# Opening of a decoder trunk's first layer: loads and transposes by token block, squares and their sums one block later

## The chip, the cores and the metric

The kernel runs on one core of a Trainium2 chip. Its time is the device time of one execution in microseconds (us). Three runs of the kernel before gave 2376.44 us as their median, from 2374.88 to 2378.19.

## The reference, cut to what matters

The program is one inference step of a two-layer decoder for 1024 prompt tokens and 8 sample tokens (1032 columns in the kernel), with a model width of 1024. The first layer (layer A) is a gated linear recurrence, and each layer ends in an MLP. What the change touches is the start of layer A and the start of both MLPs:

```
def rmsnorm(x, g):
    y = xf * lax.rsqrt(jnp.mean(xf * xf, axis=-1, keepdims=True) + EPS)
    return (y * g.astype(jnp.float32)).astype(x.dtype)

h = rmsnorm(x, g_mix[layer])
q, f, i, g = jnp.split(h @ w_in, [hk, 2 * hk, 2 * hk + hv], axis=-1)
forget = lb + (1.0 - lb) * jax.nn.sigmoid(f.astype(f32))
log_f = jnp.log(forget)          # lb comes from a_lb
...
x = x + sq_relu_mlp(rmsnorm(x, g_mlp[layer]), w_up[layer], w_down[layer])
```

The kernel moves the gain g into the weights and multiplies by the root R of the mean square after the product, since R is one number per token.

## The kernel before, in words

Activations lie with features on partitions and tokens in the free dimension. A float32 product is made of three float32r products of upper and lower parts: upper weight by upper activation, lower weight by upper, upper weight by lower. The upper part is made by ScalarE (ACT) as a rounded copy, the lower by VectorE (DVE) as the difference. A "job" is one 128-column block of a weight against all 1032 tokens: 8 slices k by 3 products are 24 steps, each of three matmuls of 344 columns (72 matmuls). One job reads one weight tile of 512 KB (`wr`), which becomes 16 parts in the tile `w` (lines 190 and 191; 195 and 198 where there is no gain).

The order of PE, DVE and ACT is written out by hand: each engine works through its list in the order in which the Python code calls it. `mix_at` (line 344) walks the steps of a job and calls the items of a side list at their step numbers; after each step it takes one waiting weight part from `pend`. So an item with number 8 stands on its engines before step 8.

The opening (lines 873 to 901) runs thus. SP loads four blocks of x (128 tokens by 1024, 512 KB each, tile `xin`), the first weight, four more blocks, the eight sample rows and the second weight. ACT issues the loads of five rows of gains and `a_lb` (tile `setup`). PE turns the gains (line 879) and then x: `turn_x(part, k)` (line 493) makes four transposes of feature slice k into one PSUM bank, ACT and DVE make its parts (lines 503, 504). Part 0 is tokens 0 to 511, part 1 is 512 to 1023, part 2 the samples. The first job (z, the forget gate of head 0) begins with a third of its columns (`z_first`), which need part 0 alone; `z_rest` does the others. The second job is q, the third is v.

`token_stats` (line 522) gives R: ACT squares each token block of `xin` and adds up along the row (line 532), DVE puts the sums on a diagonal (`dg`, line 538), PE multiplies the diagonal by a constant matrix (line 554), ACT takes exp(-0.5 ln) (lines 435, 436) and DVE refines it in three operations (lines 429 to 431). In the kernel before, four blocks are squared in `z_rest` and five in q, and the sums, `bounds` (lines 509 to 520) and `biases` (lines 145 to 159, matmuls for attention tables of layer B) stand in q at steps 10 to 15. The z tile is copied out by ACT and multiplied by R later (line 622); q and v are multiplied by R as DVE empties PSUM (line 614). `gates` (sigmoid line 677, forget line 681, logarithm 685, keys 690, scan 694) stands in v.

Before each MLP, `last_pass` gives eight row blocks y; `done(m)` (line 950) returns for each one its parts, its square (line 951) and the running sum of squares (line 956). Those of the last block run in the first MLP job, beside `rstd_steps`: three sums on PE (line 468), two roots on ACT, two refinements on DVE. The third sum uses the spare half of a PSUM tile whose other half takes the job's third chunk.

A counter of finished transfers is waited for before it is used again: eight counters serve the transfers that SP and ACT issue, in the order of the code.

Of the kernel before, what the change touches and what calls it, by code (L numbers as in the profile page):

```python
# [17 lines left out]
P = 128  # L18
# [24 lines left out]
def trunk(ctx: ExitStack, tc: tile.TileContext, x_prompt, x_sample, state_hgrn, cache_k, cache_v,  # L43
# [56 lines left out]
    rows, rel = setup[:57, :P], setup[:33, P:P + HB + 2 * P + 1]  # L100
    rbn = setup[:33, 480:480 + P].rearrange("p (i b h) -> p i b h", i=2, h=HB // 2)
    for r0, src in ((0, g_mix), (16, g_mlp), (32, a_lb)):
        S.dma_start(out=rows[r0:r0 + 16], in_=src.rearrange("l (k p) -> (l k) p", p=P))
    S.dma_start(out=rows[48:56], in_=g_kv.rearrange("(k p) -> k p", p=P))
    S.dma_start(out=rows[56:57], in_=a_gnorm)
    xin = {}

# [7 lines left out]
    for i in range(4):  # L115
        load_x(i)
# [227 lines left out]
    def mix_at(dense, items):  # L344

        items = sorted(items, key=lambda x: x[0])
        for i, step in enumerate(dense):
            while items and items[0][0] <= i:
                items.pop(0)[1]()
            step()  # L350
            if pend:
                pend.pop(0)()
        for _, f in items:
            f()
# [133 lines left out]
    for i in range(4, NBLK + 1):  # L488
        load_x(i)
# [3 lines left out]
    def turn_x(part, k):  # L493
        o = ps()
        if part < 2:
            cs = HALF[part]
            for j in range(4):
                PE.transpose(out=o[:, blk(j)], in_=xin[part * 4 + j][:, blk(k)], identity=ident)
        else:
            cs = slice(SEQ, T)  # L500
            PE.transpose(out=o[:, :NS], in_=xin[NBLK][:NS, blk(k)], identity=ident[:NS, :NS])
        o = o[:, :cs.stop - cs.start]
        S.activation(out=xs[k][0][:, cs], in_=o, func=AF.Copy)
        V.tensor_tensor(out=xs[k][1][:, cs], in0=o, in1=f32(xs[k][0][:, cs]), op=ALU.subtract)
# [103 lines left out]

    def scaled(name, then, late=None):
# [44 lines left out]
    def head_jobs(h, late=None):  # L654
# [3 lines left out]
        def got_f(z):  # L658
            hd.k = z

        def got_q(q):
            hd.q = q

        def got_v(v):
            hd.v = v

        return hd, (job(xs, scaled("z", got_f, late)) + job(xs, scaled("q", got_q))
                    + job(xs, scaled("v", got_v)))
# [204 lines left out]
    for h in range(H):  # L873
        late = [] if h == 0 else None
        hd, dense = head_jobs(h, late)
        if h == 0:
            z_first, z_rest = first_job(scaled("z", lambda z: setattr(hd, "k", z), late))
            o = ps()
            PE.transpose(out=o[:, :57], in_=rows, identity=ident[:57, :57])
            V.tensor_copy(out=cols, in_=o[:, :57])  # L880
            want_w(1)
            for k in range(NK):
                turn_x(0, k)
                pend.pop(0)()
            for k, f in enumerate(z_first):
                f()
                if k > 4:
                    turn_x(1, k - 5)
            for k in range(NK):
                if k > 2:  # L890
                    turn_x(1, k)
                turn_x(2, k)
            squares, diagonal, sums, refine = token_stats()
            mix_at(z_rest, spaced(squares[:4], 11, 25) + spaced(diagonal[:3], 15, 25))
            side = spaced(squares[4:], 0, 7) + spaced(diagonal[3:], 1, 9)
            side += list(zip((10, 10.1, 10.2, 11, 12.5, 12.6), sums + refine))
            side += [(1, load_biases), (14, bounds), (15, biases), (20, lambda: late[0]())]
            mix_at(dense[3 * NK:6 * NK], side)
            loads.close()
            mix_at(dense[6 * NK:], spaced(gates(hd), 1, 20))  # L900
# [32 lines left out]
    def last_pass(ins, ys, g=None):  # L933
# [11 lines left out]
        def done(m):  # L945
# [11 lines left out]
            if m == NK - 1:  # L957
                return [(1, square), (2, upper), (3, total), (5, lower)]
# [117 lines left out]
    def mlp(layer, ys, side, final=None):  # L1076
# [25 lines left out]
        for g in range(NG):  # L1102
            us, rs, pairs = [], [], []
            quads = g < NG - 1
            for e in mlp_order(g):
# [16 lines left out]
                if g == 0 and n == 0:  # L1122
                    spare = []
                    dense = job(xs, up_evac(rs), spare=spare)
                    at = side + list(zip((7.5, 8, 8.5, 9.5, 10, 10.5, 12), stats.rstd_steps(spare)))
# [456 lines left out]
```

## Time and profile before

| | |
|---|---|
| median of three runs | 2376.44 us |
| the profiled execution | 2374.52 us |
| its span, first to last instruction | 2372.8 us |
| PE busy | 2322.2 us, 98% of the span |
| DVE busy | 1622.6 us, 68% |
| ACT busy | 937.9 us, 40% |
| mean granted clock of TensorE | 0.995 |

The profiled execution is one run of the program with the hardware profiler. Its times count from the start of the span. PE is busy nearly all the time, so what costs time is where it waits, and where its granted clock is 0.50 (1.2 GHz) and not 1.00 (2.4 GHz). Idle time of another engine matters only where PE waits for it. A number in square brackets at the end of a timeline row is the idle time of the engine just before, and what ended it.

### The profile page before, as it was taken

The numbers are of one execution on the slowest core, as the hardware profiler recorded it, in microseconds if no ns is written. First come the engines' busy times: TensorE is split into PE (matmuls) and PEld (weight loads), VectorE is DVE, ScalarE is ACT, GpSimd is POOL, SyncE is SP. The second block draws the span as 40 slices with busy tenths as digits, with TensorE's granted clock in tenths as the row PEclk, the third lists the DMA queues.
The fourth block names the chain that finished last, engine by engine and source line by source line (L and its number), as shares of the span: only waits on it lengthen the run. The fifth ranks groups of instructions, "written<-read, shape, count | busy, mean of one in ns | idle before, by whom it ended". The sixth has DMA issues, their size and how long they took to land. (4 is left out here: it accounts for less than half of the span.)

```text
span 2372.8 us, 40040 instructions
## 1 busy us (share of the span) xinstructions
PE 2322.2 (98%) x16371; PEld 2288.1 (96%) x16371; DVE 1622.6 (68%) x3122; ACT 937.9 (40%) x1911; POOL 207.2 (9%) x209
## 2 busy tenths in 40 slices
PE   7999999999999999999999999999999999999998
PEld 6999999999999999999999989899999999999998
DVE  5766676675567667676676788886477676676765
ACT  6344454553323223223224588753222322322322
POOL 0111111120000000000000134430000000000002
PEclk8999999999999999999999999999999999999999
DMA  3222222226111111111111113011111121111122
GB/s 126 59 69 68 68 65 64 64 63 83 45 45 45 54 45 53 56 45 54 45 54 54 48 38 109 21 35 37 44 54 45 45 57 49 47 54 45 45 63 81
DMA packets 201771, 133.10 MB, mean 56 GB/s; under 512 B 10438, under 2 KB 194928, under 8 KB 201588
## 3 DMA queue, kind: packets, MB, share of 16 engines
q1 hardware_dynamic: 190740, 111.23, 16.0%
q0 software_dynamic: 10496, 18.72, 3.6%
q8 instruction: 129, 2.11, 0.4%
q10 hardware_dynamic: 352, 0.59, 0.1%
q14 instruction: 54, 0.44, 0.1%
HBM read 115.97 MB, written 14.50 MB: 55 GB/s over the span
## 5 line engine op out<-in xcount | busy, mean ns | idle before, releaser
L392 PE MATMUL ps<-h,w 128*128 128x344 f32 (+1 forms) x6096 | 1152.9, 323 | 13.0 <-DVE tmp L430 4.4
L392 PEld LDWEIGHTS ps<-h,w 128*128 128x128 f32 x6096 | 988.1, 189 | 20.7 <-issue 8.8
L392 PE MATMUL ps<-l,w 128*128 128x344 f32 (+1 forms) x3048 | 656.1, 323 | 0.0
L392 PEld LDWEIGHTS ps<-l,w 128*128 128x128 f32 x3048 | 509.1, 189 | 1.1 <-issue 0.2
L1072 DVE TENSOR_TENSOR y<-ps,y 128x516 f32<-128x516 f32 x392 | 271.6, 693 | 125.0 <-PE ps L1067 123.0
L1081 DVE SCALAR_TENSOR_TENSOR r<-ps,R 128x688 f32<-128x688 f32 x126 | 81.7, 690 | 213.3 <-PE ps L392 213.3
L1067 PE MATMUL ps<-l,w 128*128 128x258 f32 x1120 | 226.0, 283 | 0.0
L1067 PE MATMUL ps<-b,w 128*128 128x258 f32 x1568 | 225.3, 283 | 0.0
L1067 PE MATMUL ps<-t,w 128*128 128x258 f32 x1344 | 218.1, 284 | 0.0
L228 ACT ACTIVATE w<-wr 128x512 fp32r<-128x512 f32 x168 | 99.3, 623 | 292.2 <-DVE wr L240 218.2
L1087 ACT ACTIVATE r<-r 128x1032 f32<-128x1032 f32 x63 | 67.3, 1068 | 372.9 <-DVE r L1081 372.9
L1067 PEld LDWEIGHTS ps<-b,w 128*128 128x128 f32 x1568 | 205.5, 190 | 0.0
L1067 PEld LDWEIGHTS ps<-t,w 128*128 128x128 f32 x1344 | 184.8, 190 | 0.3
L1067 PEld LDWEIGHTS ps<-l,w 128*128 128x128 f32 x1120 | 173.6, 189 | 0.0
L195 ACT ACTIVATE w<-wr 128x512 fp32r<-128x512 f32 x168 | 102.5, 622 | 132.5 <-PE ps L1067 66.5
L198 DVE TENSOR_TENSOR w<-wr,w 128x512 fp32r<-128x512 f32 x168 | 116.3, 711 | 53.1 <-ACT w L195 53.0
L191 DVE SCALAR_TENSOR_TENSOR w<-wr,cols,w 128x128 fp32r<-128x128 f32 x352 | 131.7, 416 | 29.0 <-ACT w L190 28.1
L236 DVE TENSOR_TENSOR w<-wr,w 128x512 fp32r<-128x512 f32 x168 | 115.4, 687 | 42.7 <-ACT w L228 42.7
L240 DVE TENSOR_TENSOR wr<-wr 128x256 f32<-128x256 f32 x280 | 118.2, 422 | 6.2
L190 ACT ACTIVATE w<-wr,cols 128x128 fp32r<-128x128 f32 x352 | 115.5, 391 | 13.4 <-PE ps L392 12.1
L1022 ACT ACTIVATE t<-r 128x1032 fp32r<-128x1032 f32 x56 | 59.7, 1065 | 91.4 <-DVE r L1044 91.4
L1522 POOL TENSOR_TENSOR sqc<-sqc,sq 128x384 f32<-128x384 f32 (+1 forms) x18 | 16.6, 925 | 748.4 <-ACT sq L1521 748.2
(285 smaller groups left out, 2734.1 us busy)
## 6 DMA issues: line engine op xcount, KB each, us to landing
wr<-in_w_up_dram SPq DMA_DIRECT2D x64, 512.0 KB, 4.1
wr<-in_w_down_dram SPq DMA_DIRECT2D x112, 256.0 KB, 3.1
wr<-in_w_a_in_dram SPq DMA_DIRECT2D x32, 512.0 KB, 4.2
xin<-in_x_prompt_dram SPq DMA_DIRECT2D x8, 512.0 KB, 7.1
si<-in_state_hgrn_dram POOLq DMA_DIRECT2D x8, 512.0 KB, 5.0
vb<-vrows POOLq DMA_DIRECT2D x8, 512.0 KB, 3.9
out_dram<-si POOLq DMA_DIRECT2D x8, 512.0 KB, 4.2
wr<-in_w_a_out_dram SPq DMA_DIRECT2D x8, 512.0 KB, 20.9
```

Of the source, the lines that this page charges most:

```text
L190: S.activation(out=hi[:, j], in_=part[:, j], func=AF.Copy, scale=g[:, k:k + 1])
L191: V.scalar_tensor_tensor(out=lo[:, j], in0=part[:, j], scalar=g[:, k:k + 1], in1=f32(hi[:, j]), op0=ALU.mult, op1=ALU.subtract)
L195: S.activation(out=hi, in_=part, func=AF.Copy)
L198: V.tensor_tensor(out=lo, in0=part, in1=f32(hi), op=ALU.subtract)
L228: S.activation(out=hi, in_=src, func=AF.Copy)
L236: V.tensor_tensor(out=lo, in0=src, in1=f32(hi), op=ALU.subtract)
L240: return lambda: V.tensor_tensor(out=out, in0=in0, in1=in1, op=op)
L392: PE.matmul(st["o"][c], lhsT=ww[:, col:col + P], rhs=xx[:, cs], start=((k, i) == first and also is None), stop=((k, i) == last))
L1067: PE.matmul(o[:, c, :CQ], lhsT=ww, rhs=xx[:, c * CQ:(c + 1) * CQ], start=(begins and k == 0 and i == 0), stop=(k == 1 and i == 2), skip_gr ...
L1072: V.tensor_tensor(out=y, in0=o[:, :, :CQ], in1=y, op=ALU.add)
L1081: V.scalar_tensor_tensor(out=v(r), in0=p, scalar=0.0, in1=v(R), op0=ALU.max, op1=ALU.mult)
L1087: S.activation(out=rs[-1], in_=rs[-1], func=AF.Square)
```

## The change

In the opening: SP issues the first block of x, then the first weight, then seven blocks, the samples and the second weight. ACT issues one row of gains (`first`) before the table load; the others (`load_gains`) stand after the turning of `first`. All parts of the first weight are made before the parts of x. PE turns part 0 block by block, eight transposes from one block into eight banks. Parts 1 and 2 are turned between the steps of `z_first` and `z_rest`. All nine squares stand in q (steps 0 to 8), with `hold=10`, which keeps the parts of v's weight until step 10. The sums, `bounds` and refinements stand in v; z and q are both copied out by ACT and multiplied by R in v; `biases` stands at step 22 of v and the turning of the other gains at step 22 of q.

In both MLPs: the square of the last block moves to step 0, its sum to 2.5, its upper part to 3.5; the three sums stand before step 9 instead of 8 and 9, the roots at 9, the refinements before steps 10 and 11.

```diff
-    for r0, src in ((0, g_mix), (16, g_mlp), (32, a_lb)):
-        S.dma_start(out=rows[r0:r0 + 16], in_=src.rearrange("l (k p) -> (l k) p", p=P))
-    S.dma_start(out=rows[48:56], in_=g_kv.rearrange("(k p) -> k p", p=P))
-    S.dma_start(out=rows[56:57], in_=a_gnorm)
+    first = A(F32, "setup0")[:16, :P]
+    S.dma_start(out=first, in_=g_mix.rearrange("l (k p) -> (l k) p", p=P))
+    def load_gains():
+        for r0, src in ((16, g_mlp), (32, a_lb)):
+            S.dma_start(out=rows[r0 - 16:r0], in_=src.rearrange("l (k p) -> (l k) p", p=P))
+        S.dma_start(out=rows[32:40], in_=g_kv.rearrange("(k p) -> k p", p=P))
+        S.dma_start(out=rows[40:41], in_=a_gnorm)
-    for i in range(4):
-        load_x(i)
+    load_x(0)
...
-            if pend:
+            if pend and i >= hold:
                 pend.pop(0)()
...
-    for i in range(4, NBLK + 1):
+    for i in range(1, NBLK + 1):
         load_x(i)
...
+            gains(first, 0)
+            load_gains()
             want_w(1)
-            for k in range(NK):
-                turn_x(0, k)
-                pend.pop(0)()
+            while pend:
+                pend.pop(0)()
+            half = [ps() for _ in range(NK)]
+            for j in range(4):
+                for k in range(NK):
+                    PE.transpose(out=half[k][:, blk(j)], in_=xin[j][:, blk(k)], identity=ident)
+            for k in range(NK):
+                parts_x(half[k], HALF[0], k)
             for k, f in enumerate(z_first):
                 f()
-                if k > 4:
-                    turn_x(1, k - 5)
-            for k in range(NK):
-                if k > 2:
-                    turn_x(1, k)
-                turn_x(2, k)
+                if k > 3:
+                    turn_x(1, k - 4)
+                    turn_x(2, k - 4)
             squares, diagonal, sums, refine = token_stats()
...
-            side += list(zip((10, 10.1, 10.2, 11, 12.5, 12.6), sums + refine))
-            side += [(1, load_biases), (14, bounds), (15, biases), (20, lambda: late[0]())]
-            mix_at(dense[3 * NK:6 * NK], side)
+            side = spaced(squares, 0, 8) + spaced(diagonal, 1, 9) + [(6, load_biases), (22, lambda: gains(rows, 16))]
+            mix_at(dense[3 * NK:6 * NK], side, 10)
             loads.close()
-            mix_at(dense[6 * NK:], spaced(gates(hd), 1, 20))
+            side = list(zip((0.1, 0.2, 0.3, 1.5, 2, 2.1), sums + refine)) + [(2.2, f) for f in late]
+            side += [(0.4, bounds), (22, biases)]
+            mix_at(dense[6 * NK:], side + spaced(gates(hd), 3.5, 20), 3)
...
             if m == NK - 1:
-                return [(1, square), (2, upper), (3, total), (5, lower)]
+                return [(0, square), (2.5, total), (3.5, upper), (5, lower)]
...
-                    at = side + list(zip((7.5, 8, 8.5, 9.5, 10, 10.5, 12), stats.rstd_steps(spare)))
+                    at = side + list(zip((8.2, 8.3, 8.4, 8.5, 8.6, 9.5, 10.5), stats.rstd_steps(spare)))
```

ACT at the start of the program, before. The five loads into `setup` stand without a wait, and the parts of x (`h`) alternate with those of the first weight (`w`).

```order
L103 DMA setup_73<-in_g_mix_dram 16x128
L103 DMA setup_73<-in_g_mlp_dram 16x128
L103 DMA setup_73<-in_a_lb_dram 16x128
L104 DMA setup_73<-in_g_kv_dram 8x128
L105 DMA setup_73<-in_a_gnorm_dram 1x128
L117 ACT_TABLE_LOAD
L503 ACTIVATE h_119<-ps_162 128x512 [waits PE_49]
L190 ACTIVATE w_160<-wr_105,cols 128x128 [waits DMAHW1_49,DVE_49]
```

The same place in the changed kernel, and below it PE's first transpose of each block of x, which names the counter of that block: blocks 1 to 4 use DMAHW3 to DMAHW6.

```order
L103 DMA setup_2_74<-in_g_mix_dram 16x128
L126 ACT_TABLE_LOAD
L108 DMA setup_73<-in_g_mlp_dram 16x128 [waits DMAHW3_49]
L108 DMA setup_73<-in_a_lb_dram 16x128 [waits DMAHW4_49]
L109 DMA setup_73<-in_g_kv_dram 8x128 [waits DMAHW5_49]
L110 DMA setup_73<-in_a_gnorm_dram 1x128 [waits DMAHW6_49]
L199 ACTIVATE w_161<-wr_96,cols 128x128 [waits DMAHW2_49,DVE_49]
L199 ACTIVATE w_161<-wr_96,cols 128x128 x3
```

```order
L892 MATMUL ps_179<-ident,xin_76 128x128 [waits DMAHW1_49]
L892 MATMUL ps_179<-ident,xin_98 128x128 [waits DMAHW3_49]
L892 MATMUL ps_179<-ident,xin_100 128x128 [waits DMAHW4_49]
L892 MATMUL ps_179<-ident,xin_102 128x128 [waits DMAHW5_49]
L508 MATMUL ps_253<-ident,xin_104 128x128 [waits DMAHW6_49,PE_49]
```

The last four loads of ACT now stand behind the counters of blocks 1 to 4 and ahead of every part of the first weight; PE needs block 4 itself (`xin_104`) only in `z_first`.

DVE in q, before: the small operations of `biases` (lines 147 and 149, on `setup`) follow `bounds`, and z times R (line 622) comes after them.

```order
L520 TENSOR_SCALAR oml<-lb 128x8 [waits DVE_49]
L147 TENSOR_SCALAR setup_73<-setup_73 33x64 [waits DMAHW3_49,DMAHW2_49]
L147 TENSOR_SCALAR setup_73<-setup_73 33x64
L149 TENSOR_SCALAR setup_73<-setup_73 33x16 [waits DVE_49]
L155 COPY bias_s<-ps_554 64x258 [waits PE_49]
L156 COPY nsk<-ps_554 128x16
L159 COPY vrow<-ps_560 16x128 [waits PE_49]
L622 TENSOR_TENSOR z_425<-z_425,R_496 128x1032
```

DVE in v, in the changed kernel: z and q times R (line 637), forget (687), keys (696), the scan (700), and then the same small operations.

```order
L637 TENSOR_TENSOR z_417<-z_417,R_557 128x1032 [waits DVE_49]
L637 TENSOR_TENSOR q_542<-q_542,R_557 128x1032
L200 SCALAR_TENSOR_TENSOR w_549<-wr_547,cols,w_549 128x128 [waits DMAHW1_49,Activation_49]
L200 SCALAR_TENSOR_TENSOR w_549<-wr_547,cols,w_549 128x128 [waits Activation_49] x3
L687 TENSOR_SCALAR z_417<-z_417,oml,lb 128x1032
L200 SCALAR_TENSOR_TENSOR w_550<-wr_547,cols,w_550 128x128 [waits Activation_49] x4
L693 COPY fs_650<-z_417 128x8 [waits DVE_49]
L696 TENSOR_SCALAR z_417<-z_417 128x1032 [waits DVE_49,Activation_49]
L700 SCALAR_TENSOR_TENSOR b_671<-m_137,lf_648 128x1024
L156 TENSOR_SCALAR setup_73<-setup_73 33x64 [waits DMAHW3_49,DMAHW2_49]
L156 TENSOR_SCALAR setup_73<-setup_73 33x64
L158 TENSOR_SCALAR setup_73<-setup_73 33x16 [waits DVE_49]
```

The matmuls of `biases` on PE wait for these operations, and they moved from ahead of the gates to behind the scan.

ACT at the start of the first MLP, before: the upper part of one half of the next weight (`w_5990`) stands ahead of the square of the last block (`sq_5998`).

```order
L951 ACTIVATE sq_5951<-y_5530 128x1032
L195 ACTIVATE w_5990<-wr_5988 128x512 [waits DMAHW2_49,PE_49,Activation_49]
L951 ACTIVATE sq_5998<-y_5576 128x1032 [waits DVE_49,Activation_49]
L195 ACTIVATE w_5991<-wr_5988 128x512 [waits PE_49,Activation_49]
L415 ACTIVATE h_6004<-y_5576,cols 128x1032 [waits Activation_49]
```

The same place in the changed kernel.

```order
L964 ACTIVATE sq_5956<-y_5535 128x1032
L964 ACTIVATE sq_5993<-y_5581 128x1032 [waits DVE_49,Activation_49]
L204 ACTIVATE w_5997<-wr_5995 128x512 [waits DMAHW2_49,PE_49]
L204 ACTIVATE w_5998<-wr_5995 128x512 [waits PE_49,Activation_49]
L425 ACTIVATE h_6018<-y_5581,cols 128x1032 [waits Activation_49]
```

The square and the upper part of the weight changed places. On DVE the order did not change: the lower part of that weight stands before the sum of squares in both kernels.

```order
L955 TENSOR_TENSOR y_5581<-ps_5947,y_5581 128x344 [waits PE_49]
L207 TENSOR_TENSOR w_5997<-wr_5995,w_5997 128x512 [waits DMAHW2_49,Activation_49]
L969 TENSOR_TENSOR sq_5651<-sq_5651,sq_5993 128x1032 [waits DVE_49]
L207 TENSOR_TENSOR w_5998<-wr_5995,w_5998 128x512 [waits Activation_49]
L433 SCALAR_TENSOR_TENSOR l_6023<-y_5581,cols,h_6018 128x1032 [waits DVE_49,Activation_49]
```

So on DVE the sum of squares (line 969) now has, through the lower part ahead of it, the later upper part of ACT as its condition.

## Rows read from the trace of the kernel before

**Rows 1.** Waits of PE, whole program: us in total, times, longest.
```profile
PE ps L392 <- DVE tmp L430: 4.4, 2, 2.2
```
**Rows 2.** Stretches: length, busy time by engine, granted clock (PEclk), DMA.
```profile
44.30:57.90 13.60, 10.12 (x37) 8.93 (x36) 7.33 (x23) 7.05 (x16) 0.00 (x0) 0.50 0.13 38
575.30:579.30 4.00, 0.00 (x0) 0.00 (x0) 3.94 (x5) 0.98 (x2) 0.00 (x0) 1.00 0.51 128
579.40:583.50 4.10, 4.10 (x17) 4.04 (x18) 2.87 (x4) 2.63 (x3) 0.00 (x0) 0.59 0.14 33
1665.60:1669.00 3.40, 2.88 (x10) 2.88 (x11) 0.99 (x2) 0.00 (x0) 0.00 (x0) 0.50 0.00 0
```
**Rows 3.** Waits of SP's DMA queue, 0 to 120 us.
```profile
SPq L111 <- DMA setup<-in_g_mix_dram: 1.6, 1, 1.6
```
**Rows 4.** Timeline of the opening: start, us, engine, line, tiles, count [idle before].
```profile
11.26 6.16 PE L498 MATMUL ps<-ident,xin 128*128 128x128 f32 x29 [1.88 <-DMA xin<-in_x_prompt_dram]
13.08 0.40 ACT L190 ACTIVATE w<-wr,cols 128x128 fp32r<-128x128 f32 x1 [0.71 <-DVE l L504]
13.38 0.58 ACT L503 ACTIVATE h<-ps 128x512 fp32r<-128x512 f32 x1
17.17 0.56 PE L643 MATMUL ps<-h,w 128*128 128x344 f32 x2
26.90 2.44 ACT L190 ACTIVATE w<-wr,cols 128x128 fp32r<-128x128 f32 x8
```
**Rows 5.** Timeline from the squares to the end of v.
```profile
29.25 1.05 ACT L532 ACTIVATE junk<-xin 128x1024 f32<-128x1024 f32 x1
33.84 1.14 ACT L618 ACTIVATE z<-ps 128x344 f32<-128x344 f32 x3
42.39 0.66 ACT L435 ACTIVATE r<-ps,eps_t 128x512 f32<-128x512 f32 x1
43.84 0.69 DVE L429 SCALAR_TENSOR_TENSOR tmp<-r 128x512 f32<-128x512 f32 x1 [0.68 <-ACT r L436]
50.32 1.09 PE L152 MATMUL ps<-setup 33*64 33x129 f32 x4 [3.48 <-ACT w L190]
52.41 2.09 PE L392 MATMUL ps<-h,w 128*128 128x344 f32 x6
52.73 1.21 DVE L622 TENSOR_TENSOR z<-z,R 128x1032 f32<-128x1032 f32 x1
53.97 1.06 ACT L677 ACTIVATE z<-z 128x1032 f32<-128x1032 f32 x1 [3.10 <-DVE z L622]
55.04 1.28 ACT L131 ACT_TABLE_LOAD   x1
59.14 1.36 DVE L614 TENSOR_TENSOR q<-ps,R 128x344 f32<-128x344 f32 x3 [5.20 <-PE ps L392]
61.73 0.81 DVE L681 TENSOR_SCALAR z<-z,oml,lb 128x1032 f32<-128x1032 f32 x1
63.67 2.27 DVE L690 TENSOR_SCALAR z<-z 128x1032 f32<-128x1032 f32 x1 [0.26 <-ACT lf L685]
65.86 2.28 DVE L694 TENSOR_TENSOR_SCAN b<-m,lf 128x1024 f32<-128x1024 bf16 x1
70.48 1.36 DVE L614 TENSOR_TENSOR v<-ps,R 128x344 f32<-128x344 f32 x3 [2.34 <-PE ps L392]
```
**Rows 6.** Timeline of the first MLP's start.
```profile
606.13 0.68 DVE L198 TENSOR_TENSOR w<-wr,w 128x512 fp32r<-128x512 f32 x1
607.41 1.23 DVE L956 TENSOR_TENSOR sq<-sq,sq 128x1032 f32<-128x1032 f32 x1 [0.60 <-ACT sq L951]
607.28 0.61 ACT L195 ACTIVATE w<-wr 128x512 fp32r<-128x512 f32 x1
608.79 1.39 PE L468 MATMUL ps<-sq,ones_d 128*128 128x344 f32 x4 [1.22 <-DVE sq L956]
615.93 0.89 PE L392 MATMUL ps<-h,w 128*128 128x344 f32 x4 [2.23 <-DVE tmp L430]
```

More of the change, by code (lines that the diff above doesn't have):

```diff
@@ L99, in trunk, with gains @@
     setup = A(F32, "setup")
-    rows, rel = setup[:57, :P], setup[:33, P:P + HB + 2 * P + 1]
+    rows, rel = setup[:41, :P], setup[:33, P:P + HB + 2 * P + 1]
     rbn = setup[:33, 480:480 + P].rearrange("p (i b h) -> p i b h", i=2, h=HB // 2)
-    for r0, src in ((0, g_mix), (16, g_mlp), (32, a_lb)):
-        S.dma_start(out=rows[r0:r0 + 16], in_=src.rearrange("l (k p) -> (l k) p", p=P))
-    S.dma_start(out=rows[48:56], in_=g_kv.rearrange("(k p) -> k p", p=P))
-    S.dma_start(out=rows[56:57], in_=a_gnorm)
+    first = A(F32, "setup0")[:16, :P]
+    S.dma_start(out=first, in_=g_mix.rearrange("l (k p) -> (l k) p", p=P))
     xin = {}
+    def load_gains():
[3 more added lines that the diff above has]
+        S.dma_start(out=rows[40:41], in_=a_gnorm)
+    def gains(src, c0):
+        n = src.shape[0]
+        o = ps()
+        PE.transpose(out=o[:, :n], in_=src, identity=ident[:n, :n])
+        V.tensor_copy(out=cols[:, c0:c0 + n], in_=o[:, :n])
     def load_x(i):
@@ L342, in mix, with mix_at @@
             step()
-    def mix_at(dense, items):
+    def mix_at(dense, items, hold=0):
         items = sorted(items, key=lambda x: x[0])
@@ L501, in turn_x, with parts_x @@
             PE.transpose(out=o[:, :NS], in_=xin[NBLK][:NS, blk(k)], identity=ident[:NS, :NS])
-        o = o[:, :cs.stop - cs.start]
+        parts_x(o[:, :cs.stop - cs.start], cs, k)
+    def parts_x(o, cs, k):
         S.activation(out=xs[k][0][:, cs], in_=o, func=AF.Copy)
@@ L607, in trunk, with got @@
         pass
+    def got(hd, key):
+        return lambda t: setattr(hd, key, t)
     def scaled(name, then, late=None):
@@ L656, in head_jobs @@
         hd.h = h
[L658 to L668, printed above, removed]
+        return hd, (job(xs, scaled("z", got(hd, "k"), late)) + job(xs, scaled("q", got(hd, "q"), late))
+                    + job(xs, scaled("v", got(hd, "v"))))
     def gates(hd, other=None):
@@ L876, in trunk @@
         if h == 0:
[L877 to L880, printed above, removed]
+            z_first, z_rest = first_job(scaled("z", got(hd, "k"), late))
+            gains(first, 0)
+            load_gains()
             want_w(1)
+            while pend:
+                pend.pop(0)()
+            half = [ps() for _ in range(NK)]
@@ L893, in trunk @@
-            squares, diagonal, sums, refine = token_stats()
-            mix_at(z_rest, spaced(squares[:4], 11, 25) + spaced(diagonal[:3], 15, 25))
-            side = spaced(squares[4:], 0, 7) + spaced(diagonal[3:], 1, 9)
-            side += list(zip((10, 10.1, 10.2, 11, 12.5, 12.6), sums + refine))
-            side += [(1, load_biases), (14, bounds), (15, biases), (20, lambda: late[0]())]
-            mix_at(dense[3 * NK:6 * NK], side)
+                if k > 3:
+                    turn_x(1, k - 4)
+                    turn_x(2, k - 4)
@@ L899, in trunk @@
+            squares, diagonal, sums, refine = token_stats()
+            for i, f in enumerate(z_rest):
+                f()
+                if i % 3 == 0 and i < 12:
+                    turn_x(1, 4 + i // 3)
+                    turn_x(2, 4 + i // 3)
+                if i > 11 and pend:
+                    pend.pop(0)()
+            side = spaced(squares, 0, 8) + spaced(diagonal, 1, 9) + [(6, load_biases), (22, lambda: gains(rows, 16))]
+            mix_at(dense[3 * NK:6 * NK], side, 10)
             loads.close()
-            mix_at(dense[6 * NK:], spaced(gates(hd), 1, 20))
+            side = list(zip((0.1, 0.2, 0.3, 1.5, 2, 2.1), sums + refine)) + [(2.2, f) for f in late]
```

## The prediction

> **What bounds the kernel now.** I began with the waits of PE and the stretches of low clock, since PE is busy for 98% of the span. A kernel like this loses time in two ways: PE waits, or PE works at 0.50 of its clock. The waits show, in the part that the change touches, the first steps of the two MLPs, 2.2 us each, for the last operation of the root R [rows 1]. The stretches show where the clock is low: from 44.3 to 57.9 us the mean granted clock is 0.50, while PE is busy for only 10.1 of 13.6 us; after a wait of 4.0 us (575.3 to 579.3) it is 0.59 over the next 4.1 us; and in the second MLP's start it is 0.50 for another 3.4 us [rows 2]. Then I read the timelines of the opening, of layer A's first three jobs and of the MLP's start, to see which wait ends last at each point. What follows goes by four marks: S, the first product of the z job (17.17 us before [rows 4]); Z, the end of z (its copy begins at 33.84); the end of v (its first copy begins at 70.48); and the resumption of PE in the MLP (615.93) [rows 5, 6].
>
> **The start, up to S.** The change takes x's parts out of the alternation with the weight's parts and turns x block by block. It also moves ACT's last four small loads ahead of all weight parts, and the order of the changed kernel gives them a wait for the counters of x's blocks 1 to 4. A queue that has to issue a load stands still until the counter is there: SP waited 1.6 us in that way for g_mix [rows 3]. If ACT does the same, no weight part is made before block 4 is there. Block 4 is the sixth large transfer (x0, w0, x1, x2, x3, x4). Before, the fourth one had landed at 11.26 at the latest, since PE began on it then, and the fifth, the weight, at 13.08, when ACT made its first part [rows 4]. So the sixth lies between 13.1 and 13.08 + 1.8 = 14.9; I take the middle, 14.0. From there: 0.3 to pass the waits, the eight upper weight parts 2.44, one upper part of x 0.58 [rows 4], its lower part 0.69 (as the 512-wide DVE operation of [rows 5]). S = 14.0 + 0.3 + 2.44 + 0.58 + 0.69 = 18.0, which is 0.8 later than before; with the ends of the landing, 17.1 to 18.9.
>
> From S to Z stand 72 matmuls and 40 transposes of blocks 4 to 8. The job before v's end had 72 matmuls between the copies of q at 59.14 and of v at 70.48, 11.3 us [rows 5]. A transpose took 6.16 / 29 = 0.21 us in the opening [rows 4]; at the full clock I put it at half, so 40 take 4.0. That is 15.3, and if ACT and DVE hold the transposes back a little, 16.2; I take 15.7. PE has nothing to do for some 3.7 us ahead of S, so the first matmuls may run at the low level; that costs 0 to 1.2, and I take 0.8. Z = 18.0 + 15.7 + 0.8 = 34.5, against 33.8: **+0.7**, bounds -0.7 to +2.0.
>
> **From Z to the end of v.** Before, this took 70.48 - 33.84 = 36.6 us [rows 5]. It held the matmuls of two jobs, a wait of 3.5 us ahead of the matmuls of `biases`, and the 13.6 us at half clock. In the changed kernel the squares and weight parts are apart, and q runs densely: 72 matmuls, v begins at about Z + 12. What is late next is `biases`. Its matmuls now stand on PE ahead of step 22 of v, and the small DVE operations that they read stand on DVE behind the scan, as the order shows. PE can't pass them, and the rest of v, two steps and its copy, is queued behind.
>
> The chain that ends there begins on ACT at Z: copy of z 1.14, nine squares at (33.84 - 29.25) / 4 = 1.15 each (before, four stood between these two rows), 10.3 [rows 5]; eight weight parts of v, 2.44 [rows 4], made behind the squares; copy of q 1.14, four roots and exponentials of 0.66 and 0.8 between them [rows 5]. That is Z + 18.4. Then DVE: six refinements of 0.69 with 1.0 of gaps and the tail of `bounds` 0.5, 5.5 in all, and z times R 1.21, Z + 25.1; on ACT the sigmoid 1.06 and the table load 1.28, and three weight parts 0.9, Z + 28.4; on DVE a lower weight part 0.3, forget 0.81, four more lower parts and the small copy 1.3, keys 2.27, scan 2.28, Z + 35.4, and 0.4 for the three small operations: Z + 35.8 [rows 5].
>
> PE reaches step 22 earlier: 12 to the start of v, 22 steps of 11.3 / 24 = 0.47 are 10.4, the sums of R some 2.2 (six at 1.39 / 4 = 0.35 [rows 6]), and up to 1.0 for a bank; Z + 25.6. So it stands idle for about 10 us, which is a wait that the kernel before doesn't have. The matmuls of `biases` begin at 50.32 and the next products at 52.41, 2.1 later, at half clock [rows 5]; the two steps left are 0.94 at full clock and 1.7 or so at half. After a wait of 4.0 us the clock was low [rows 2], so after 10 I take it as low. End of v: Z + 35.8 + 2.1 + 1.7 = Z + 39.5, against Z + 36.6: +2.9. The job after it starts at the low level too: the loss in the row after the 4.0 us wait is 4.1 x (1 - 0.59), 1.7 us in all [rows 2], of which about 1.2 are spent inside `biases` and the two steps, and 0.5 is left. **+3.4**, bounds +0.9 (the clock doesn't fall) to +4.4.
>
> **The two MLPs.** On ACT the square changes places with an upper weight part (0.61), so the square is ready some 0.6 earlier. The sum of squares on DVE still stands behind the lower part of that weight (0.68), which now waits for an upper part that comes after a 1.1 us square. Before: the upper part, the lower part at 606.13, its end at 606.81, a wait of 0.60 for the square, the sum at 607.41 [rows 6]. After: the square ends 0.6 earlier, at about 606.8; upper part 0.61 and lower part 0.68, then the sum at 608.5 to 608.6, 1.2 later. From the sum on, the chain is what it was: sum's end 607.41 + 1.23 = 608.64, PE resumes at 615.93, 7.3 later [rows 6], and all its links (sums, roots, refinements) are in the change. But PE is now held one step earlier: the refinements stand before steps 10 and 11, and the third chunk that needs the spare half stands at step 11 rather than 12; one step more, 0.47, is left for after. Each opening +1.2 + 0.4 = 1.6, so **+3.2** for two. To this comes the clock: the wait grows from 2.2 to 3.9 us, and the row of the second MLP shows 3.4 us at 0.50, of which PE's 2.88 busy us lose about 1.4 [rows 2]. If the first MLP too falls to that level, another 1.4: I take **+1.4**, bounds 0 to 2.9.
>
> **The sum.** 0.7 + 3.4 + 3.2 + 1.4 = +8.7 us on the profiled execution's own 2374.52, or 2383.2. That execution is 1.9 below the median of the runs shown; against the median it would be 2385.1, and I forecast 2383. What can be told from no change is about 0.2%, 4.75 us: faster is below 2371.7, slower above 2381.2. Nothing else in the program changes its order by a price that I can read; a different place of buffers may add or take 2 us.
>
> **Rivals.** *The loads don't hold ACT.* The row that I go by is of SP; no row shows ACT waiting at an issue. If the waits are passed on, the weight's parts start when the weight lands, at about the landing of the second large transfer, S is set by x's block 3 at 11 to 12 us and its parts, about 15.5, and Z falls by 2.5: 2383.2 - 2.5 = 2380.6. Against it: the loads and the weight parts are in one list of one engine.
>
> The Trainium skill has a sentence on this in "DMA: Bandwidth & Descriptors", section "Anatomy of one DMA", the gpsimd path: "any semaphore wait happens on the issuing sequencer before dispatch." It is written for another path than ACT's; by it the loads hold ACT and the sum stays at 2383, and SP's 1.6 us [rows 3] agree.
>
> *The clock stays full.* Then the terms of the clock go, 0.8 + 0.8 + 0.5 + 1.4 + the 1.2 of `biases` = 4.7: 2378.5. For it: ahead of 575.3 the clock was full, and a wait of 2.2 us in the first MLP is not in the rows of low clock. Against it: the 4.0 us wait was followed by the low level [rows 2], and mine is longer.
>
> *The MLP part does nothing* (the change doesn't do what it says there, the one move being paid by the other): 2383.2 - 4.6 = 2378.6. For it: 0.6 us of DVE's idle time ahead of the sum are free today [rows 6]. Against it: the lower part still has to come first.
>
> *The other side: `biases` holds nobody.* The place is PE's step 22 of v. If the DVE chain is some 10 us shorter than I make it, because squares or weight parts run beside other things in ways my chain puts end to end, it is through when PE gets there at Z + 25.6. The wait, its low clock and the 13.6 us at half clock of before are all gone: v ends at Z + 29, 7.6 earlier than before, and with the opening's +0.7, the MLPs' +4.6 and a full clock the sum is 2374.5 + 0.7 - 7.6 + 4.6 = 2372.2, or 2371 with an early S. It decides from a chain of less than Z + 29: then each us less than that is a gain. Against it: keys, scan, forget, sigmoid and table load alone are 7.7 us [rows 5] behind R, which needs all nine squares behind Z.
>
> **How the numbers follow.** My forecast (+5 to +13 us) has 0.53; the loads rival 0.12, the full clock 0.14, the MLP rival 0.10, the other side 0.11. The forecast lies above 2381.2 in 0.47 and below in 0.06; the loads rival is split in halves; of the full clock and of the MLP rival 0.03 each are slower and the rest is no change; the other side is 0.09 faster, 0.02 no change; and 0.01 of the others may be faster. That makes faster 0.10, no change 0.31, slower 0.59. The range goes from 2375 (the full clock and the MLP rival with 3.5 us off) to 2390 (every bound of the sum at its upper end: 2.0 + 4.4 + 3.2 + 2.9 = +12.5 is 2387, and 2 to 3 more for what the sum doesn't hold).
>
> **What would show it.** In the changed kernel's waits: one of PE for DVE at `biases` in v of about 10 us (under 3 would make the second term wrong and the other side right), and no wait of 3.5 us in q. In its timeline: the first upper weight part at 14 us and S at 18 (S at 15.5 would be the loads rival). In the MLP: PE resuming 1.6 us later, with the wait at 3.9. In the stretches: low clock behind `biases`; a full one would be that rival. A time under 2375 makes the prediction wrong, and most of all its 10 us.

## The result, and the profile after

The changed kernel took 2389.32 us, the median of four runs (2387.8 to 2392.32); the kernel before took 2377.06 in the runs beside it. The ratio is 1.0054, with a 95% interval of 1.0037 to 1.0072: slower, by 9 to 17 us. The profiled execution took 2387.8 us, with a span of 2386.1 against 2372.8.

Waits of PE in the changed kernel (us in total, times, longest); the row of `tmp` answers to [rows 1]:

```profile
PE ps L161 <- issue: 9.7, 1, 9.7
...
PE ps L402 <- DVE y L955: 4.4, 1, 4.4
PE ps L402 <- DVE tmp L440: 4.4, 2, 2.2
PE ps L658 <- DVE l L516: 4.0, 1, 4.0
...
PE ps L402 <- ACT r L445: 2.9, 2, 1.4
```

The 9.7 us stand ahead of the bias matmuls (line 161), where the kernel before waited 3.5 us [rows 5]. The 4.0 us stand ahead of the first product. The profile names "issue" as the cause of the long one: PE's instruction waits for two tiny operations on DVE (line 156), and only the timeline shows what these stood behind.

Timeline of the changed kernel's opening (start, us, engine, line, tiles, count, idle time before and what ended it); these rows answer to [rows 4, 5]. ACTq is the queue from which ACT issues its loads; the first row is the last of its four small ones:

```profile
14.09 0.23 ACTq L110 DMA_DIRECT2D setup<-in_a_gnorm_dram  x1
14.43 2.44 ACT L199 ACTIVATE w<-wr,cols 128x128 fp32r<-128x128 f32 x8 [11.88 <-DMA xin<-in_x_prompt_dram]
18.13 0.94 PE L658 MATMUL ps<-h,w 128*128 128x344 f32 x2 [3.99 <-DVE l L516]
...
38.14 1.10 PE L402 MATMUL ps<-h,w 128*128 128x344 f32 x6
...
50.41 1.05 PE L566 MATMUL ps<-dg,ones_d 128*128 128x128 f32 x8
...
52.74 0.66 ACT L445 ACTIVATE r<-ps,eps_t 128x512 f32<-128x512 f32 x1
...
71.08 2.28 DVE L700 TENSOR_TENSOR_SCAN b<-m,lf 128x1024 f32<-128x1024 bf16 x1
73.28 0.26 DVE L156 TENSOR_SCALAR setup<-setup 33x64 f32<-33x64 f32 x2
...
73.54 1.09 PE L161 MATMUL ps<-setup 33*64 33x129 f32 x4 [9.71 <-issue]
...
77.18 1.36 DVE L629 TENSOR_TENSOR v<-ps,R 128x344 f32<-128x344 f32 x3 [1.17 <-PE ps L402]
...
91.40 1.36 DVE L629 TENSOR_TENSOR z<-ps,R 128x344 f32<-128x344 f32 x3 [5.14 <-PE ps L402]
```

Read it by points that both kernels have. The first product of q stood at 34.08 us before, the copy of the next head's z at 83.06:

```profile
34.08 1.10 PE L392 MATMUL ps<-h,w 128*128 128x344 f32 x6
...
83.06 1.36 DVE L614 TENSOR_TENSOR z<-ps,R 128x344 f32<-128x344 f32 x3 [4.58 <-PE ps L392]
```

So the changed kernel is 4.1 us late when z ends (38.14), 6.7 at v's copy (77.18 against 70.48 [rows 5]) and 8.3 at the next z (91.40). The granted clock explains the odd tenths. Stretches of the changed kernel (length, busy time of PE, PE's loads, DVE, ACT, POOL, then PEclk):

```profile
18.10:23.40 5.30, 5.27 (x20) 5.04 (x20) 4.16 (x7) 2.64 (x6) 0.00 (x0) 0.53 0.53 141
...
73.50:79.00 5.50, 5.46 (x20) 4.65 (x21) 2.61 (x9) 0.40 (x2) 0.00 (x0) 0.50 0.00 0
79.00:82.00 3.00, 3.00 (x15) 3.00 (x15) 1.62 (x5) 2.54 (x8) 0.00 (x0) 0.65 0.02 5
...
627.20:630.60 3.40, 3.40 (x14) 3.40 (x13) 0.00 (x0) 0.00 (x0) 0.00 (x0) 0.51 0.02 5
```

After each of the two long waits PE works at the low level for some microseconds: by the granted clock, 5.3 x 0.47 = 2.5 us are lost behind the first product. The last row is the first MLP, which ran at the full level before. Its timeline, which answers to [rows 6]:

```profile
617.51 1.23 DVE L969 TENSOR_TENSOR sq<-sq,sq 128x1032 f32<-128x1032 f32 x1
...
618.89 1.97 PE L478 MATMUL ps<-sq,ones_d 128*128 128x344 f32 x6 [1.18 <-DVE sq L969]
...
622.60 0.91 PE L402 MATMUL ps<-h,w 128*128 128x344 f32 x4 [1.43 <-ACT r L445]
...
626.02 0.42 PE L402 MATMUL ps<-l,w 128*128 128x344 f32 x1 [2.20 <-DVE tmp L440]
...
633.54 1.30 DVE L1094 SCALAR_TENSOR_TENSOR r<-ps,R 128x688 f32<-128x688 f32 x2 [7.02 <-PE ps L402]
```

Set against the last copy of y ahead of it (604.93 before, 613.90 after), the sum of squares is 1.1 us later, and the first copy of the up product 3.1 later (621.42 before). In the second MLP the same copy moves from 1672.92 to 1686.19, and the copy of y ahead of it from 1655.12 to 1666.67: 1.7. The sum of all: 4.1 + 2.6 + 1.6 + 3.1 + 1.7 = 13.1 of the 13.3 us between the two spans; what comes and goes between (0.6 later at the first output block, 0.6 earlier before the second MLP) cancels.

### The profile page after: what moved, and what is told of

The parts are those of the page before. It is cut to its first block, busy times and chain, and to the rows that moved or that the text cites. A ratio compares the mean times of both kernels' runs of the same rounds, so it can differ in the third digit from the quotient of the medians.

```text
span 2386.1 us, 40037 instructions
## 1 busy us (share of the span) xinstructions
PE 2325.2 (97%) x16372; PEld 2290.4 (96%) x16372; DVE 1620.7 (68%) x3121; ACT 939.2 (39%) x1914; POOL 207.4 (9%) x209
## 5 line engine op out<-in xcount | busy, mean ns | idle before, releaser
L402 PEld LDWEIGHTS ps<-h,w 128*128 128x128 f32 x6096 | 988.5, 189 | 18.1 <-issue 9.6
L200 DVE SCALAR_TENSOR_TENSOR w<-wr,cols,w 128x128 fp32r<-128x128 f32 x352 | 129.0, 410 | 36.8 <-ACT w L199 35.8
```

The lines of the kernel that those rows point to most:

```text
L200: V.scalar_tensor_tensor(out=lo[:, j], in0=part[:, j], scalar=g[:, k:k + 1], in1=f32(hi[:, j]), op0=ALU.mult, op1=ALU.subtract)
L402: PE.matmul(st["o"][c], lhsT=ww[:, col:col + P], rhs=xx[:, cs], start=((k, i) == first and also is None), stop=((k, i) == last))
```

## The experiments

Each run's time is a median, and the ratio is to the kernel before, run on the same chip (2375.8 to 2376.4). The changed kernel was not run again beside them, and the kernel before had given 2377.1 beside it: where a run is set against 2389.3, a difference of 1 to 2 us is not settled by the times, and I go by the trace.

**The MLP part alone, both ways.** In the first run the changed kernel has the MLPs of before; in the second the kernel before has the changed MLPs.

```
-                return [(0, square), (2.5, total), (3.5, upper), (5, lower)]
+                return [(1, square), (2, upper), (3, total), (5, lower)]
...
-                    at = side + list(zip((8.2, 8.3, 8.4, 8.5, 8.6, 9.5, 10.5), stats.rstd_steps(spare)))
+                    at = side + list(zip((7.5, 8, 8.5, 9.5, 10, 10.5, 12), stats.rstd_steps(spare)))
```

> The changed kernel (2389.3 us) with the two MLP openings as they were before; all else as changed. Theory: the moved square makes the sum of squares 1.1 us later, and PE takes up full speed later, 3.1 us in the first MLP and 1.7 in the second; so 4.8 us come back, 2384.5, and the sum starts 2.5 us after the last y again, not 3.6. Rival: in the first MLP the low clock comes from elsewhere (the opening's pushed-back weights), and only the 1.1 us of each is the MLP's; then 2.2 come back, 2387.

> The kernel before (2376) with the MLP part of the change alone. Theory: the sum of squares 1.1 us later in each MLP, and low clock behind PE's longer wait in both: 3.3 in the first and 1.5 in the second, 4.8 in all, 2380.8. Rival: by itself, without the opening, the clock doesn't fall; then 2.2, 2378. It also tells if the two parts of the change add up: 2389.3 less this difference should be what the changed kernel with the old MLPs took, 2387.

Measured: 2387.03 for the first (2381.59 to 2390.58), and 2381.34 for the second (ten runs; ratio 1.0022, 1.0013 to 1.0031). The second settles the size: +4.9 us, with an interval of 3 to 7. Its stretch from 618 to 619 us is at 0.50, so the clock falls without the opening's help. The first run, at 2.3 less than the changed kernel, is scattered over 9 us; its median does not tell 4.8 from 2.2, nor whether the two parts of the change add up. In its profiled execution the first MLP's waits for the sum and the root are 0.7 and 0.5 us, against 1.2 and 1.4 in the changed kernel, and the clock is full in both MLPs. The last row is a stretch of the second one:

```profile
PE ps L402 <- DVE tmp L440: 2.2, 1, 2.2
PE ps L478 <- DVE sq L969: 0.7, 1, 0.7
PE ps L402 <- ACT r L445: 0.5, 1, 0.5
```

```profile
1673.00:1676.50 3.50, 2.04 (x13) 2.04 (x14) 1.82 (x4) 0.00 (x0) 0.00 (x0) 1.00 0.00 0
```

From the last copy of y to the first copy of the up product it takes 16.5 us in each MLP; the changed kernel took 19.6 and 19.5, the kernel before 16.5 and 17.8. So in this execution 6.1 us came back, 1.3 of them because the second MLP stayed at the full level where the kernel before did not.

**ACT's loads behind the parts of x.** The call of `load_gains` moves down nine lines.

```
-            load_gains()
...
                 parts_x(half[k], HALF[0], k)
+            load_gains()
```

> The changed kernel with ACT's last four small loads moved behind the parts of x's first half; all else as changed. Theory: these loads held ACT until block 4 of x had landed; without them the weight parts are made while x lands, the first product is set by block 3's transposes (end 14.1) and comes at 15.5 instead of 18.1; PE stands for 1.4 us, not 4.0, ahead of it, so the low clock of 18.1 to 23.4 (2.5 us) goes too. z ends 2.6 to 5.1 earlier, and the whole is 2384.2 to 2386.7. Rival: ACT waited for something else (the weight's landing); the first product stays at 18, the time at 2389.

Measured: 2384.14, 5.2 less than the changed kernel (ratio 1.0036, 1.0023 to 1.0049). The weight's parts begin at 6.31 us, when the weight has landed, and the first product comes at 14.26 after a wait of 0.65, at the full clock; q's first product comes 5.5 us earlier, at 32.64. Timeline, then the stretches:

```profile
6.31 2.44 ACT L199 ACTIVATE w<-wr,cols 128x128 fp32r<-128x128 f32 x8 [3.76 <-DMA wr<-in_w_a_in_dram]
...
14.26 0.58 PE L658 MATMUL ps<-h,w 128*128 128x344 f32 x2 [0.65 <-DVE l L516]
```

```profile
18.10:23.40 5.30, 5.30 (x35) 4.47 (x35) 3.34 (x9) 3.06 (x10) 0.00 (x0) 1.00 0.47 113
```

So the loads did hold ACT: with them ahead, the first part was made at 14.43, just behind the issue of the last one at 14.09, which waits for the counter of block 4.

**PE kept at work ahead of the first product.**

```
+            for _ in range(2):
+                for k in range(NK):
+                    PE.transpose(out=half[k][:, blk(3)], in_=xin[3][:, blk(k)], identity=ident)
             for k in range(NK):
                 parts_x(half[k], HALF[0], k)
```

> The changed kernel with 16 more transposes of x's block 3 (the same ones again, over the same results), which fill most of PE's 4.0 us wait ahead of the first product. Theory: the low clock from 18.1 to 23.4 comes from that wait; with PE at work the first product stays at 18.1 but runs at the full clock, z ends 2.5 us earlier, the whole at 2386.8. Rival: the clock is low there for another reason (the change from transposes to products); then nothing changes, 2389.3, or it is later by what the transposes take.

Measured: 2387.26 (1.0051, 1.0036 to 1.0066), 2.1 less, which the two intervals do not tell from nothing. The trace does: the first product comes at 17.81, after an idle time of 1.08 us and not 3.99, the stretch from 18.1 to 23.4 is at the full level, and q's first product comes 2.4 us earlier than in the changed kernel (38.14):

```profile
17.81 0.58 PE L658 MATMUL ps<-h,w 128*128 128x344 f32 x2 [1.08 <-DVE l L516]
...
35.75 1.10 PE L402 MATMUL ps<-h,w 128*128 128x344 f32 x6
```

```profile
18.10:23.40 5.30, 5.30 (x35) 4.60 (x34) 4.92 (x10) 3.65 (x9) 0.00 (x0) 1.00 0.43 120
```

The low clock behind the first product is the price of the idle time ahead of it. From the first product of z to that of q it took 17.9 us here and 20.0 in the changed kernel: the price is 2.1 us.

**The bias matmuls moved out of v, and then the scan too.** First run; the second adds the lines of the second piece.

```
-            side += [(0.4, bounds), (22, biases)]
+            side += [(0.4, bounds)]
...
+            if h == 1:
+                side += [(40, biases)]
```

```
-            mix_at(dense[6 * NK:], side + spaced(gates(hd), 3.5, 20), 3)
+            g = gates(hd)
+            mix_at(dense[6 * NK:], side + spaced(g[:3], 3.5, 13.4) + [(30, g[3]), (31, g[4])], 3)
```

> The changed kernel with the bias matmuls and their small DVE operations moved from step 22 of v to step 40 of the next head's jobs; all else as changed. Theory: PE's wait of 9.7 us at that place and the low clock behind it (2.3 inside the bias matmuls and last steps, 1.6 behind) are the cost; v's copy comes at 65 us and not at 77.2, and the whole at 2389.3 - 13.9 = 2375.4. Rival: something else of the same chain (the scan and what the next head's jobs need of it) holds PE some 10 us later, and most is given back: 2385 or more, with a new wait of PE between 66 and 100 us.

> The run with the bias matmuls moved (2391.4), with keys and scan put behind v's copy on DVE; all else as in that run. Theory: PE's 8.6 us wait at v's transposes is for DVE's queue, where v's copy stood behind keys and scan (4.7 us); the copy then starts at 68.7, the wait is some 4 us, and the whole 2391.4 - 4.7 = 2386.7. Rival: PE meets the chain again one step later, in the next head, and the gain is given back: 2390 or more.

Measured: 2391.37 and 2389.40; neither is better than the changed kernel. In the first my theory fell, and the rival held: PE reached the end of v early, but v's own copy stood on DVE behind the same scan, and the transposes of v waited for it. In the second the copy came early and the wait shrank as expected, but of the 4.7 us hoped for the medians show 2.0. Timeline of the first run:

```profile
71.21 2.28 DVE L700 TENSOR_TENSOR_SCAN b<-m,lf 128x1024 f32<-128x1024 bf16 x1
73.42 1.33 DVE L629 TENSOR_TENSOR v<-ps,R 128x344 f32<-128x344 f32 x3
...
73.95 1.11 PE L721 MATMUL ps<-ident,v 128*128 128x128 f32 x4 [8.60 <-DVE v L629]
```

With the scan behind the copy that wait fell to 3.9, but the wait at the bias matmuls, in both runs in the next head, grew from 2.2 to 5.1 us. Of the 3.8 and 9.9 us won at v's copy, nothing and 1.9 were left at the next head's copy of q. Waits of the second run from 50 to 110 us:

```profile
PE ps L161 <- issue: 5.1, 1, 5.1
PE ps L721 <- DVE v L629: 3.9, 1, 3.9
```

**Fewer squares behind z.**

```
+                if i > 19:
+                    squares[i - 20]()
-            side = spaced(squares, 0, 8) + spaced(diagonal, 1, 9) + ...
+            side = spaced(squares[4:], 0, 4) + spaced(diagonal, 0.5, 5) + ...
```

> The changed kernel with the first four squares back beside the end of the z job (its last four steps) and the other five at q's steps 0 to 4; all else as changed. Theory, after the run with the bias matmuls moved: not the bias matmuls but the chain squares, roots, R, gates, scan, all behind z on ACT and DVE, is 10 us late, and PE meets it wherever it first needs DVE. Four squares of 1.18 us less behind z make PE's wait in v 9.7 - 4.7 = 5.0 us, and the whole 2389.3 - 4.7 = 2384.6. Rival: the chain's end is set by v's weight parts or the table loads, not by the squares; the wait stays at 9 to 10, the time at 2389.

Measured: 2387.95, and PE's wait is what it was, to a hundredth:

```profile
48.45 2.45 ACT L199 ACTIVATE w<-wr,cols 128x128 fp32r<-128x128 f32 x8 [0.88 <-issue]
...
49.95 1.05 PE L566 MATMUL ps<-dg,ones_d 128*128 128x128 f32 x8
...
51.82 0.68 ACT L445 ACTIVATE r<-ps,eps_t 128x512 f32<-128x512 f32 x1
...
72.64 1.09 PE L161 MATMUL ps<-setup 33*64 33x129 f32 x4 [9.72 <-issue]
```

The gain that I expected did not come, but the run moves less than it was meant to: ACT began the first of the four squares at 36.08, only 1.7 us ahead of q's first product, and all nine ended at 47.6, 1.9 us earlier than in the changed kernel (49.5) and not 4.7. Behind them two bounds are left. The sums of R are the third job's, so on PE they stand behind all of q, and begin at 49.95 (50.41 in the changed kernel) whenever the squares end. And ACT is busy without a break from 48.45 to the first root at 51.82, with v's weight parts and the copy of q. The second bound is the rival that I had named, and this run does not tell it from the first; the run with the sums in v, below, does.

**A version from these runs, and its parts.** It takes the loads behind the parts of x and the old MLPs, does three squares while x lands and four between the last transposes, and has the sums back in q:

```
+            squares[0]()
             want_w(1)
...
+            squares[1]()
+            squares[2]()
             half = [ps() for _ in range(NK)]
...
+                if i in (4, 7, 10, 13):
+                    squares[3 + i // 3 - 1]()
...
+            side = spaced(squares[7:], 0, 2) + [(1.5, diagonal[7]), (2.5, diagonal[8])]
+            side += list(zip((7, 7.1, 7.2, 10, 11, 11.1), sums + refine))
+            side += [(1, load_biases), (6, lambda: gains(rows, 16)), (13, bounds), (16, lambda: late[0]())]
+            mix_at(dense[3 * NK:6 * NK], side, 3)
...
+            mix_at(dense[6 * NK:], spaced(gates(hd), 1, 20))
...
+            if h == 1:
+                side += [(20, biases)]
```

> A version from what the runs showed: the changed opening with ACT's four loads behind the parts of x's first half, squares of blocks 0 to 2 while x lands, four more between the transposes of z's second part, two at q's start; the sums of R in q at step 7 and z times R at 16; q multiplied by R as it leaves PSUM; gates in v as before; the bias matmuls at step 20 of the next head's jobs; the MLPs as before. Theory: no wait of 10 us, as the gate chain runs beside v, and v's copy comes at 58 to 60 us (70.5 before, 77.2 after), so the whole is 10 to 12 us under the kernel before, 2364 to 2366, and 1 or 2 less if no stretch of low clock is left there. Rival: the squares between the transposes hold PE back, or the sums wait for them, by 5 us or more: 2370 or more.

Measured: 2371.02 (ratio 0.9975, 0.9966 to 0.9985), 5.4 under the kernel before, where I expected 10 to 12. The opening did nearly what was expected: v's copy at 60.43 (58 to 60 expected), 10.05 us earlier than before. Of this 7.2 us are left at the copy of the next head's z; in between lie the bias matmuls, 2.0 us of waiting at v's transposes and some low clock (0.53 from 61 to 64 us); then it shrinks in places that no edit touches. Two runs change one thing of this version. The first puts the sums, and what follows them (roots, refinements, z and q times R, and the gates from step 3.5), back into v; the second puts the bias matmuls back at step 22 of v.

```
-            side += list(zip((7, 7.1, 7.2, 10, 11, 11.1), sums + refine))
...
+            side = list(zip((0.1, 0.2, 0.3, 1.5, 2, 2.1), sums + refine)) + [(2.2, f) for f in late]
```

```
-            mix_at(dense[6 * NK:], spaced(gates(hd), 1, 20))
+            mix_at(dense[6 * NK:], spaced(gates(hd), 1, 20) + [(22, biases)])
```

> The version of 2371.0 us with one thing as in the changed kernel: the sums of R and all that follows them (roots, refinements, z and q times R, bounds) in the third job, v; the squares stay early, the bias matmuls in the next head. Theory, after the run with four squares moved left PE's wait at 9.7: the chain to the scan begins at the sums, which stand on PE behind all of q, so early squares alone are worth nothing; v's transposes wait for DVE some 8 us again, and with the low clock behind it the time is 2379 to 2382. Rival: the squares on ACT are what makes the chain late; then nothing is lost, 2371 to 2373.

> The version of 2371.0 us with the bias matmuls back at step 22 of v, as the change has them. Theory: with the chain early the scan ends at 60.4 us, PE reaches that step at 57.9; so the wait there is 2.5 to 3 us in place of the 2.0 at v's transposes, and the time is 2371 to 2373: the place of the bias matmuls alone is worth 2 us or less. Rival: the place alone is what costs; a wait of 5 us or more comes back, 2376 or more.

Measured: 2380.67 (2374.64 to 2383.77) with the sums in v, 2373.33 with the bias matmuls in v. The first is as expected, the second 0.3 above it. With the sums in v all squares end at 37 us and v's weight parts at 39.5, ACT waits 0.52 us for the sums, and PE still waits for v's copy; so here it is the place of the sums that makes the chain late, and not ACT's work. With the bias matmuls in v PE waits a third of the 9.7 us. The sums and the first root with the sums in v, then one wait of each run:

```profile
45.36 2.26 PE L566 MATMUL ps<-dg,ones_d 128*128 128x128 f32 x18
...
46.45 0.69 ACT L445 ACTIVATE r<-ps,eps_t 128x512 f32<-128x512 f32 x1 [0.52 <-PE ps L566]
```

```profile
PE ps L721 <- DVE v L629: 8.4, 1, 8.4
```

```profile
PE ps L161 <- issue: 3.1, 1, 3.1
```

The place of the sums is worth 9.7 us between medians, that of the bias matmuls 2.3. (The profiled execution with the sums in v is the fastest of its nine; I take only its waits.)

**Two more that beat both kernels.** The version above with keys and scan behind v's copy; and the kernel before with nothing but its bias matmuls moved.

```
+            g = gates(hd)
+            mix_at(dense[6 * NK:], spaced(g[:3], 1, 12) + [(30, g[3]), (31, g[4])])
```

```
-            side += [(1, load_biases), (14, bounds), (15, biases), (20, lambda: late[0]())]
+            side += [(1, load_biases), (14, bounds), (20, lambda: late[0]())]
...
+            if h == 1:
+                side += [(20, biases)]
```

> The version of 2371.0 us with keys and scan behind v's copy on DVE. Theory: the last wait of this stretch, 2.0 us at v's transposes, and 1 us of low clock behind it go; 2368. Rival: the next head meets the later scan, or the gain is taken back at the first output block, where PE waited 5.3 us in that version and 4.0 before; 2371.

> The kernel before with one edit: the bias matmuls moved from step 15 of q to step 20 of the next head's jobs. Theory: PE's wait of 3.5 us in q goes, and some of the 13.6 us at half clock there; 2370 to 2372, about what the longer rebuilding of the opening gave. Rival: PE meets the roots and bounds one step later all the same, as with the changed kernel; 2375 or more.

Measured: 2366.30 (0.9962, 0.9949 to 0.9974), a little better than expected, and 2370.24 (0.9977, 0.9969 to 0.9986), as expected. The first is the fastest of all; PE is busy without a gap and at the full level through the whole stretch where the changed kernel idled:

```profile
44.00:58.00 14.00, 14.00 (x91) 14.00 (x90) 9.76 (x29) 7.47 (x14) 1.90 (x1) 1.00 0.20 52
58.00:70.00 12.00, 12.00 (x79) 11.16 (x78) 9.37 (x19) 6.67 (x16) 0.57 (x1) 1.00 0.23 65
70.00:82.00 12.00, 12.00 (x78) 11.77 (x78) 9.31 (x16) 6.42 (x11) 5.86 (x4) 1.00 0.18 61
```

The second, one item of a list, wins as much as the rebuilt opening before its last edit. It takes away the 3.5 us wait [rows 5] and most of the half clock (0.90 from 44 to 58 us, against 0.50 over 13.6 us [rows 2]).

## Why the prediction was right, point by point

The direction, the places and the length of the chain held; 2383 was forecast and 2389.3 measured, inside the range, near its end. Against the profiled execution the sum was +8.7, the span grew by 13.3.

- **The start, up to S: right.** The first weight part was put at 14.3 and S at 18.0; they came at 14.43 and 18.13. That the loads hold ACT was tested by moving them. So the first rival falls.
- **From S to Z: mis-sized, and most of the error.** The term for Z was +0.7, and by q's first product Z came 4.1 later. From S to Z I had 15.7 + 0.8 = 16.5 us, and it took 20.0. Two things failed. The size of the 72 products and 40 transposes: with PE kept at work, and the clock full throughout, they took 17.9 and not 15.7. I had put them together from pieces and halved the 0.21 us of a transpose for the full clock, but the row I took it from was at the full clock already:

```profile
11.26:17.17 5.91, 5.91 (x30) 5.91 (x30) 4.22 (x9) 4.69 (x12) 0.00 (x0) 1.00 1.05 380
```

The kernel before had the whole of it, 34.08 - 17.17 = 16.9: 1.2 of the 2.2 could have been read there, and 1.0 came with the new order. And the low clock behind the idle time, put at 0.8 with a bound of 1.2, cost 2.1.
- **From Z to the end of v: right in size, half right in cause.** The inputs of the bias matmuls were put at Z + 35.8, and the matmuls began 35.4 behind q's first product (73.54 - 38.14); PE was to wait 10 and waited 9.7. The term was 2.9 to v's copy and 0.5 behind it; measured are 2.6 and 1.6, as the low clock lasted longer. But the step "what is late next is `biases`" names only the place where PE meets the chain. Moving the bias matmuls or the scan moved the wait. From the first root to the end of the scan it is 20.6 us in the changed kernel, 20.6 with four squares moved and 20.7 with the sums in v; so what counts is when the first root can run. I had let that follow from ACT's list alone (nine squares, weight parts, copy of q), and left out that the sums of R stand on PE behind all of q. In the changed kernel the two bounds lie close together by chance: the sums begin at 50.41, and ACT is through with its list at 52.74. That neither helps when taken alone is shown for the squares only in part (1.9 us), and for the sums it is an argument: they need the last square, at 49.5.
- **The MLPs: right in size, in part by luck.** The sum was +4.6, and is 4.8 in the profile, 4.9 between medians of the run with that part alone. The later sum was priced rightly (1.2, measured 1.1), and so was the fall of the first MLP to the low level, 3.0 in all against 3.1; the second, which had been there before, has 1.7 against 1.6. Its place was wrong: I had the wait for the last refinement grow from 2.2 to 3.9. The rows name the second of the three refinements (line 440, before 430), and that wait stayed 2.2, while the wait for the root (line 445) grew from 0.5 to 1.4. The luck is in the clock, which does not follow from the waits alone (see the end): the profile of the run with the MLPs put back differs from that of the changed kernel by 6.1 us there.
- **The rivals.** The clock did not stay full, the MLP part did not do nothing, and the bias matmuls did hold PE. The other side would have needed the sums in q: the versions that have them there, with squares done early enough, are the ones that are faster.

## What to carry to other kernels

When PE waits for a small operation on another engine, ask what that operation stands behind, and follow it back to the first instruction that is placed and not merely late; where the chain behind it is late, moving the waiting matmul only moves the wait (the changed kernel); where the chain is early, it can take the wait away (the kernel before, 6 us). A quantity that many later steps need (here R) goes as early as its inputs allow, on each engine it passes, since taking away one of two bounds that lie close together gives little. And where both kernels have the same stretch, take its length from the trace as a whole before building it from pieces.

## What the runs showed that I had not expected

The low clock need not begin when PE comes back. In the first MLP of the changed kernel PE waited 1.2, 1.4 and 2.2 us in turn, resumed at 626.02 at the full level, and fell to the low one at 627.2, where it stayed for 3.4 us (0.51). With waits of 1.2, 0.5 and 2.2 the kernel before stayed at the full level throughout. But the waits alone do not decide it. The kernel before with its bias matmuls moved has the same 1.2, 0.5 and 2.2 there, resumed at 609.08, and fell:

```profile
609.50:612.90 3.40, 3.40 (x16) 3.40 (x15) 0.08 (x1) 0.00 (x0) 0.00 (x0) 0.58 0.02 5
```

In the second MLP, waits of 0.5 and 2.2 were followed by 3.4 us at 0.50 in the kernel before [rows 2], and by the full level in the changed kernel with the MLPs put back. What else decides is open.

And time won early is partly lost again, in part by this. In the profiled executions the version with one item moved is 6.95 us ahead of the kernel before at 76 us, 6.85 at the last copy of y ahead of the first MLP, 5.3 at the first copy of the up product, and 4.6 at the end.
